# Rotary embedding: two DMA pieces merged with their neighbours, and two PSUM banks per ScalarE copy

## The chip, the cores and the metric

The kernel runs on one core of one Trainium2 chip. The metric is the device time of one execution, in microseconds. Executions over 1.5% slower than the fastest of the same kernel are left out of the means. A ratio in this document is the mean time of one kernel's fast runs over the mean of the other's fast runs in the same rounds, so it is not quite the ratio of the medians that stand beside it.

## The reference

```python
# x: (8, 2048, 8, 64) float32; cos, sin: (2048, 32) float32
x1, x2 = x[..., :32], x[..., 32:]
out1 = x1 * cos - x2 * sin          # cos, sin broadcast over batch and heads
out2 = x1 * sin + x2 * cos
return np.concatenate([out1, out2], axis=-1)
```

The kernel reads 33.5 MB of `x` and 0.5 MB of tables, and writes 33.5 MB.

## The kernel before

Each of the 8 batches is one SBUF tile of 128 partitions by 8192 floats (4 MB, 32 KB a partition), and five such tiles rotate. A batch is worked on in four units of 1 MB, some of them cut in halves. For a unit, GpSimd (POOL) makes `t2`, the products with the sine, and VectorE (DVE) makes `t1`, the product with the cosine; then DVE adds them in place. That is kind A. In kind B, TensorE adds the two through the identity matrix into PSUM, and ScalarE (ACT) copies the sum back; in kind C, DVE makes both products, and TensorE and ScalarE add them in the same way. Kinds B and C take the first unit of batches 1 to 5.

```python
    o_pool = ctx.enter_context(tc.tile_pool(name="op", bufs=2, space=PSUM))
    ...
    def load(b):
        xt = xpool.tile([P, ROW], f32, tag="xt", name=f"xt{b}")
        for lo, n in spans([UNIT, UNIT, 2 * UNIT] if b == 0 else [ROW]):
            keep(nc.sync.dma_start(out=xt[:, lo : lo + n], in_=xv[b, :, lo : lo + n]))
            ...  # the tables are loaded after the first piece
    ...
        if kind == "A":
            keep(nc.vector.tensor_add(out=xt, in0=t1, in1=t2))
        elif kind == "B":
            for j in range(n // C):                       # C = 512, one PSUM bank
                o = o_pool.tile([P, C], f32, tag="o")
                cs = slice(j * C, (j + 1) * C)
                nc.tensor.matmul(o, eye, t1[:, cs], start=True, stop=False)
                nc.tensor.matmul(o, eye, t2[:, cs], start=False, stop=True)
                keep(nc.scalar.copy(xt[:, cs], o))
    ...
    def pieces(b):                                        # what is computed at a time
        if b == 0:
            return [2 * HD, 2 * HD, UNIT, UNIT, UNIT]     # UNIT = 4 * HD
        if b == last:
            return [UNIT, UNIT, UNIT, 2 * HD, 2 * HD]
        return [UNIT] * 4

    def shares(b):                                        # what is stored at a time
        if b == 0:
            return [HD, 7 * HD, 2 * UNIT]
        if b == last:
            return [2 * UNIT, UNIT, UNIT]
        return [ROW]
```

## Time and profile before

| | before |
|---|---|
| time, median | 163.35 us (163.27 to 163.38) at first; 163.33 over 6 runs |
| span of the profiled run | 161.4 us |
| DVE, POOL busy | 140.1 us, 139.0 us |
| TensorE (PE), ACT busy | 46.4 us, 14.4 us |
| bytes moved, mean rate | 67.65 MB, 419 GB/s |

A busy share is a mean over the span. The 16 DMA engines each carry 8 of the 128 partitions and end at slightly different times, and the span ends with the last of them.

### The profile page before, as it was taken

The page shows a single profiled execution, that of the slowest core. Times are in us where ns is not written, and L with a number is a line of the kernel's source. Part 1 is how long each engine was busy: PE and PEld are TensorE (multiplying, and loading weights), DVE is VectorE, ACT ScalarE, POOL GpSimd, SP SyncE. Part 2 cuts the span into 40 slices and gives each one's busy share as a digit, 9 for nine tenths or more (in the row PEclk, how much of TensorE's full clock was granted, in tenths as well). Part 3 has the DMA queues.
Part 4 walks back from the last instruction along what each step waited for, and adds up shares of the span by engine and source line. Part 5 has one row for each costly group of instructions (what it writes and reads, how often), then busy time and mean ns, then how long its engine had stood idle before and what let it go on. Part 6 is the DMA issues. An engine that isn't in the chain of part 4 may idle for free.

```text
span 161.4 us, 467 instructions
## 1 busy us (share of the span) xinstructions
PE 46.4 (29%) x80; PEld 18.5 (11%) x80; DVE 140.1 (87%) x66; ACT 14.4 (9%) x24; POOL 139.0 (86%) x70
## 2 busy tenths in 40 slices
PE   0000000498008960893029912980000000000000
PEld 0000000133003420340014401430000000000000
DVE  0468899999999999999999999999899998999900
ACT  3200000013000220032001210140000000000000
POOL 1299999999999899998996999998999979999200
PEclk9999999999955696599755985799555555555555
DMA  5999999899999999999999999999999999999995
GB/s 181 418 445 464 449 430 390 373 427 499 406 390 447 430 487 390 447 438 414 447 422 430 447 416 438 447 406 447 455 392 455 447 398 455 438 406 455 410 398 231
DMA packets 3458, 67.65 MB, mean 419 GB/s; under 512 B 384, under 2 KB 384, under 8 KB 768
## 3 DMA queue, kind: packets, MB, share of 16 engines
q1 hardware_dynamic: 1728, 34.08, 49.8%
q10 hardware_dynamic: 1728, 33.56, 48.4%
q14 instruction: 2, 0.02, 0.0%
HBM read 34.08 MB, written 33.55 MB: 419 GB/s over the span
## 4 chain that ended last, share of the span: by engine, by line
DMA 46%; DVE 37%; POOL 9%; issue 2%; SPq 1%; DVEq 0%; POOLq 0%; ACTq 0%
DMA xt<-in_x_dram 24%; DVE t L128 18%; DMA out_dram<-xt 18%; DVE xt L135 17%; POOL t L121 9%; DMA sin_sb<-in_sin_dram 3%; DVE t L145 1%; SPq L69 0%; SPq L67 0%; DVEq L135 0%; POOLq L121 0%; ACTq L74 0%
## 5 line engine op out<-in xcount | busy, mean ns | idle before, releaser
L121 POOL TENSOR_TENSOR t<-xt,sin_sb 128x1024 f32<-128x1024 f32 (+1 forms) x32 | 70.4, 2200 | 10.7 <-DMA sin_sb<-in_sin_dram 5.7
L128 DVE TENSOR_TENSOR t<-xt,cos_ps 128x2048 f32<-128x2048 f32 (+1 forms) x34 | 73.4, 2166 | 0.8
L121 POOL TENSOR_TENSOR t<-xt,nsin 128x1024 f32<-128x1024 f32 (+1 forms) x32 | 70.4, 2200 | 0.0
L135 DVE TENSOR_TENSOR xt<-t,t 128x2048 f32<-128x2048 f32 (+1 forms) x29 | 62.2, 2144 | 6.2 <-POOL t L121 3.7
L140 PE MATMUL o<-t,eye 128*128 128x512 f32 x24 | 17.1, 803 | 25.2 <-DVE t L128 25.2
L156 PE MATMUL o<-t,eye 128*128 128x512 f32 x16 | 10.9, 781 | 36.8 <-DVE t L128 36.8
L141 PE MATMUL o<-t,eye 128*128 128x512 f32 x24 | 15.0, 710 | 0.0
L142 ACT COPY xt<-o 128x512 f32<-128x512 f32 x12 | 7.0, 586 | 46.5 <-PE o L141 46.5
L140 PEld LDWEIGHTS o<-t,eye 128*128 128x128 f32 x24 | 5.6, 247 | 33.5 <-issue 33.5
L161 ACT COPY xt<-o 128x512 f32<-128x512 f32 x8 | 4.7, 586 | 42.6 <-PE o L157 42.6
L156 PEld LDWEIGHTS o<-t,eye 128*128 128x128 f32 x16 | 3.6, 247 | 41.7 <-POOL t L121 30.6
L141 PEld LDWEIGHTS o<-t,eye 128*128 128x128 f32 x24 | 5.9, 248 | 8.5 <-issue 8.5
L92 DVE COPY cos_ps<-cos_sb 128x512 f32<-128x512 f32 x1 | 0.7, 695 | 6.2 <-DMA cos_sb<-in_cos_dram 6.2
L157 PE MATMUL o<-t,neye 128*128 128x512 f32 x8 | 4.9, 714 | 0.2 <-DVE t L145 0.2
L145 DVE TENSOR_TENSOR t<-xt,sin_ps 128x2048 f32<-128x2048 f32 x2 | 4.6, 2279 | 0.0
L157 PE MATMUL o<-t,eye 128*128 128x512 f32 x8 | 4.1, 592 | 0.0
L157 PEld LDWEIGHTS o<-t,neye 128*128 128x128 f32 x8 | 1.8, 239 | 3.6 <-issue 3.6
L157 PEld LDWEIGHTS o<-t,eye 128*128 128x128 f32 x8 | 1.5, 190 | 1.9 <-issue 1.9
L89 ACT ACT_TABLE_LOAD x1 | 1.3, 1283 | 0.7 <-PEq L204 0.7
L89 ACT ACTIVATE nsin<-sin_sb 128x512 f32<-128x512 f32 x1 | 0.6, 629 | 4.9 <-DMA sin_sb<-in_sin_dram 4.9
L90 ACT COPY sin_ps<-sin_sb 128x512 f32<-128x512 f32 x1 | 0.6, 580 | 0.0
L79 POOL MEMSET eye<- 128x128 f32 x1 | 0.2, 205 | 0.3 <-POOLq L204 0.3
(6 smaller groups left out, 1.0 us busy)
## 6 DMA issues: line engine op xcount, KB each, us to landing
xt<-in_x_dram SPq DMA_DIRECT2D x7, 4096.0 KB, 38.9
out_dram<-xt ACTq DMA_DIRECT2D x6, 4096.0 KB, 28.3
out_dram<-xt ACTq DMA_DIRECT2D x2, 2048.0 KB, 18.9
xt<-in_x_dram SPq DMA_DIRECT2D x2, 1024.0 KB, 6.0
xt<-in_x_dram SPq DMA_DIRECT2D x1, 2048.0 KB, 11.5
out_dram<-xt ACTq DMA_DIRECT2D x2, 1024.0 KB, 8.7
out_dram<-xt ACTq DMA_DIRECT2D x1, 1792.0 KB, 20.4
cos_sb<-in_cos_dram SPq DMA_DIRECT2D x1, 256.0 KB, 5.0
```

The source lines that it names most:

```text
L89: keep(nc.scalar.mul(nsin, sin_sb, -1.0))
L92: keep(nc.vector.tensor_copy(cos_ps, cos_sb))
L121: nc.gpsimd.tensor_mul(out=t2u[:, :, u, :].rearrange("p (r h) d -> p r h d", h=H), in0=xu[:, :, 1 - u, :].rearrange("p (r h) d -> p r h d" ...
L128: nc.vector.tensor_mul(out=t1.rearrange("p (r k d) -> p r k d", r=nr, d=Dh), in0=xk, in1=rep(cos_ps[:, r0 : r0 + nr, :], 2 * H),)
L135: keep(nc.vector.tensor_add(out=xt, in0=t1, in1=t2))
L140: nc.tensor.matmul(o, eye, t1[:, cs], start=True, stop=False)
L141: nc.tensor.matmul(o, eye, t2[:, cs], start=False, stop=True)
L142: keep(nc.scalar.copy(xt[:, cs], o))
L145: nc.vector.tensor_mul(out=t2.rearrange("p (r k d) -> p r k d", r=nr, d=Dh), in0=xk, in1=rep(sin_ps[:, r0 : r0 + nr, :], 2 * H),)
L156: nc.tensor.matmul(o, eye, t1u[:, gs, u, :], start=True, stop=False)
L157: nc.tensor.matmul(o, eye if u else neye, t2u[:, gs, 1 - u, :], start=False, stop=True)
L161: nc.scalar.copy(xu[:, gs, u, :], o.rearrange("p (g d) -> p g d", d=Dh))
```

## The change

Its intent is fewer transfers and fewer instructions: one piece less at the front, one less at the end, and half as many ScalarE copies, each of two PSUM banks. The two single-bank buffers become one of two banks. All eight banks were already in use.

```diff
-    o_pool = ctx.enter_context(tc.tile_pool(name="op", bufs=2, space=PSUM))
+    o_pool = ctx.enter_context(tc.tile_pool(name="op", bufs=1, space=PSUM))
...
-        for lo, n in spans([UNIT, UNIT, 2 * UNIT] if b == 0 else [ROW]):
+        for lo, n in spans([UNIT, 3 * UNIT] if b == 0 else [ROW]):
...
-            for j in range(n // C):
-                o = o_pool.tile([P, C], f32, tag="o")
-                cs = slice(j * C, (j + 1) * C)
-                nc.tensor.matmul(o, eye, t1[:, cs], start=True, stop=False)
-                nc.tensor.matmul(o, eye, t2[:, cs], start=False, stop=True)
-                keep(nc.scalar.copy(xt[:, cs], o))
+            for j in range(n // (2 * C)):
+                o = o_pool.tile([P, 2 * C], f32, tag="o")
+                for k in range(2):
+                    cs = slice((2 * j + k) * C, (2 * j + k + 1) * C)
+                    oc = o[:, k * C : (k + 1) * C]
+                    nc.tensor.matmul(oc, eye, t1[:, cs], start=True, stop=False)
+                    nc.tensor.matmul(oc, eye, t2[:, cs], start=False, stop=True)
+                keep(nc.scalar.copy(xt[:, 2 * j * C : 2 * (j + 1) * C], o))
...        (kind C likewise: one copy for each half of the unit)
-            return [2 * UNIT, UNIT, UNIT]
+            return [3 * UNIT, UNIT]
```

More of the change, by code (lines that the diff above doesn't have):

```diff
@@ L152, in rotate @@
             for u in range(2):
+                o = o_pool.tile([P, n // 2], f32, tag="o")
                 for j in range(n // 2 // C):
-                    o = o_pool.tile([P, C], f32, tag="o")
+                    oc = o[:, j * C : (j + 1) * C]
                     gs = slice(j * G, (j + 1) * G)
-                    nc.tensor.matmul(o, eye, t1u[:, gs, u, :], start=True, stop=False)
+                    nc.tensor.matmul(oc, eye, t1u[:, gs, u, :], start=True, stop=False)
                     nc.tensor.matmul(
-                        o, eye if u else neye, t2u[:, gs, 1 - u, :], start=False, stop=True
+                        oc, eye if u else neye, t2u[:, gs, 1 - u, :], start=False, stop=True
                     )
-                    keep(
-                        nc.scalar.copy(
-                            xu[:, gs, u, :], o.rearrange("p (g d) -> p g d", d=Dh)
-                        )
+                keep(
+                    nc.scalar.copy(
+                        xu[:, :, u, :], o.rearrange("p (g d) -> p g d", d=Dh)
                     )
+                )
     def pieces(b):
```

## The prediction

> **What bounds the kernel now.** I read the page first, for the engines, the slices, the DMA queues and the chain that ended last.
>
> ```profile
> PE 46.4 (29%) x80; PEld 18.5 (11%) x80; DVE 140.1 (87%) x66; ACT 14.4 (9%) x24; POOL 139.0 (86%) x70
> ...
> DMA  5999999899999999999999999999999999999995
> ...
> q1 hardware_dynamic: 1728, 34.08, 49.8%
> q10 hardware_dynamic: 1728, 33.56, 48.4%
> ```
>
> Two engines are near 87%, but the DMA line is at 9 in almost every slice, and the loads (q1) and stores (q10) together fill 98.2% of 16 engines' span. Of 161.4 us that is 158.5 us of packets in each DMA engine. The trace's packet records agree: their durations sum to 158.6 us for each of the 16 engines, the first data packet starts at 1.75 us and the last one ends at 160.25 us, a stretch of 158.5 us. So the DMA engines have no gap at all: **the kernel is bound by the transfer of 67.65 MB**, with 1.75 us of start before it and about 1.2 us of ending after it. The time reported, 163.35 us, is 1.9 us more than the span; I keep that offset.
>
> The chain of waits seems to say something else, since it goes through compute twice:
>
> ```profile
> DMA 46%; DVE 37%; POOL 9%; issue 2%; SPq 1%; DVEq 0%; POOLq 0%; ACTq 0%
> ```
>
> A chain names one thing at each step and does not say how much slack the others had. The slack is seen in the timeline and in the issue and packet records of each transfer. The load of batch 7 was issued at 92.68 us, when store 2 was complete, but its first packet moved only at 110.88, because loads were queued ahead of it: 18 us of slack. Stores likewise: batch 1's was issued at 46.79 and began at 53.9, batch 2's at 63.05 and 73.3, batch 6's at 133.48 and 139.9. Compute is therefore ahead of the transfers nearly everywhere.
>
> Then I read the waits of POOL, the engine that sets the pace of compute, and the windows of the end.
>
> ```profile
> POOL t L121 <- DMA sin_sb<-in_sin_dram: 5.7, 1, 5.7
> POOL t L121 <- DMA xt<-in_x_dram: 2.8, 3, 1.1
> POOL t L121 <- DVE xt L135: 1.8, 2, 1.3
> ```
>
> POOL waits for the tables once, and then three times about 0.9 us for a whole batch to land (batches 5, 6 and 7). It catches up with the loads only at the end; these 2.8 us are what a small delay at the front can be absorbed in.
>
> ```profile
> 140.00:145.00 5.00, 0.00 (x0) 0.00 (x0) 4.86 (x3) 0.00 (x0) 5.00 (x3) 0.50 1.06 459
> 145.00:148.20 3.20, 0.00 (x0) 0.00 (x0) 3.06 (x3) 0.00 (x0) 3.20 (x4) 0.50 0.95 410
> ...
> 149.60:153.30 3.70, 0.00 (x0) 0.00 (x0) 3.56 (x3) 0.00 (x0) 0.71 (x1) 0.50 0.99 425
> 153.30:156.00 2.70, 0.00 (x0) 0.00 (x0) 0.00 (x0) 0.00 (x0) 0.00 (x0) 0.50 0.96 410
> 156.00:158.00 2.00, 0.00 (x0) 0.00 (x0) 0.00 (x0) 0.00 (x0) 0.00 (x0) 0.50 1.00 422
> ```
>
> After the stretch come five busy columns (PE, PEld, DVE, ACT, POOL), the clock, the DMA share and GB/s. The DMA share is about 1 while the last batch is computed and after, so the stores have work queued until they end.
>
> **What the Trainium skill says.** (1) "DMA: Bandwidth & Descriptors", section "Bandwidth", has a 1 MB transfer at 78% of peak and a 16 MB one at 97%, with the rule to batch to at least 1 MiB. That would speak for fewer, larger pieces. This trace does not agree for queued transfers: an 8 KB packet (a 1 MB piece) takes 309 ns, a 16 KB one 611 and a 32 KB one 1213, so a piece costs about 8 ns a packet more, not 20%. The page's figure is of one transfer alone. (2) The same page, "Queues, rings and completion order", says that each engine goes round robin between the queues that have work, a packet at a time. The trace agrees: from 14.5 us load and store packets alternate, spaced 1.3 us while 2 KB stores face 32 KB loads. (3) "PSUM — Partial Sum Buffer", section "The four PSUM rules": a matmul's output stays in one bank of 512 fp32. The change keeps each matmul at 512 and lets only the copy cross banks; no trace yet shows such a copy. (4) "ScalarE: Activation LUTs", section "What ACT_TABLE_LOAD costs", gives an instruction with immediate operands as 186 ns plus 0.833 ns an element. For 512 that is 613 ns; the copies here take 586, so the measured time is a little lower.
>
> **The change part by part.**
>
> *First load, 1 and 3 MB.* Per engine it takes away 8 packets of 8 KB and 8 of 16 KB, 8 x 309 + 8 x 611 = 7360 ns, and adds 8 of 24 KB. Halfway between 611 and 1213 is 912 ns (my estimate), so 7296 ns: 64 ns less, and one semaphore packet of 9 ns less. **0.07 us of DMA time saved.** It also moves work: the second megabyte had landed at 9.0 us and POOL began on it at 11.89. The 3 MB will land where the 2 MB piece did, at 13.8 us. From landing to POOL's start took 0.6 us for batches 6 and 7 (111.75 to 112.35, 131.11 to 131.71), so POOL starts this unit at 14.4, **2.5 us late**, DVE likewise. The lines that will move are these:
>
> ```profile
> 11.89 2.33 POOL L121 TENSOR_TENSOR t<-xt,sin_sb 128x1024 f32<-128x1024 f32 x1
> ...
> 16.53 2.29 DVE L135 TENSOR_TENSOR xt<-t,t 128x2048 f32<-128x2048 f32 x1 [0.84 <-POOL t L121]
> ```
>
> What does the delay cost? The DMA engines have loads for batches 1 to 4 queued, so they do not pause. Stores of batch 0 come up to 2.5 us later, while the queues have 6 us or more of backlog from batch 1 on. The delay then shrinks at the three waits for loads, 2.8 us in all, so at batch 7 about nothing of it is left. **0 us on the end.**
>
> *Last store, 3 and 1 MB.* By the same arithmetic, 8 packets of 16 KB and 8 of 8 KB become 8 of 24 KB: **0.07 us saved**. It moves the issue of the first 2 MB from 143.42 to 148.14. Is anything else queued until then? Batch 6's store is, to between 149.6 (the first of the 16 engines to finish it) and 150.5 (the last). A transfer issued at 148.14 needs its time from issue to first packet: the first load took 1.0 us (0.74 to 1.75). It is there at about 149.15, some 0.45 us before the first engine runs dry and 1.3 us before the last. **0 us lost, with thin slack.** The last megabyte still goes out at 153.33 and is needed at 157.
>
> *Two banks per copy.* There were 20 copies of 512 columns at 586 ns, 11.7 us of ACT. There will be 10 of 1024. With the page's 0.833 ns for 512 more columns, one takes 586 + 427 = 1013 ns, 10.1 us in all: **1.6 us of ACT saved, on an engine 9% busy, so 0 us.** There is now one buffer of two banks instead of two of one, so PE waits for the copy after each pair of banks. A unit with PE had 4 tiles; it will have two rounds of 8 matmul records and a copy. PE loses one copy of 1.0 us in between, and the last copy is 0.4 us longer, plus whatever the clock costs that PE loses while it waits (853 ns a record in the first 5 us of a unit and 430 after). So such a unit ends 1.5 us later, at most some 5. The slack: PE ended batch 2's unit at 59.1, its store went out at 63.05, and the buffer that PE held is next needed by POOL two units on, again about 4 us later. **0 us on the end.**
>
> The sum: -0.07 - 0.07 + 0 + 0 = -0.15 us, rounded; 163.35 becomes **163.2 us**.
>
> **The rivals.** *A hole in the store queue at the end.* If a transfer takes much more than the 1.0 us seen for the first load from issue to first packet, the engines wait at 149.6 to 150.5. Against it stands that 1.0 us; for it that the first store was issued at 10.80 and moved its first packet at 14.51. But the loads were queued ahead in the same engines then, which they are not at the end. If 3.7 us held there too, the 3 MB would be there at 151.84 and the last engine, done at 150.48, would wait 1.4 us: some 164.6 us. With 2 us instead of 3.7 the last engine would not wait.
>
> *The late start carries to the end.* If POOL does not win its 2.5 us back, batch 7 ends up to 2.5 us later, the 3 MB goes out at 150.6 instead of 148.1, and the last engine has a hole of 150.6 + 1.0 - 150.5, about 1.1 us; 164.3 us. Against it: the three waits for loads that absorb it, and that late stores let loads run ahead for a while (round robin has fewer partners), which gives later batches their data earlier. Here the total of bytes decides, not their order.
>
> *PE as a new bound.* With one buffer PE could hold a t2 buffer past POOL's need. POOL starts already sit just at 93.0 us near PE's end of batch 4's unit (93.5), though what ended that wait by the semaphores was DVE, not PE. If the allocation of buffers now made POOL wait for PE, three units would cost up to 2 us each, and behind a backlog of stores of 6 to 10 us even this would mostly be hidden: at most 165.
>
> *Faster than the bytes.* If the fixed cost of a transfer were really 2 us (the section "Anatomy of one DMA" of the DMA page gives about that), two transfers less would be worth 4 us. But packets of following transfers already run with no gap here: that cost lies beside others' work. I give it 1%.
>
> **Range and chances.** Three runs of the kernel before lie within 0.11 us. The fast end is 163.2 less a few tenths, as if packets of 24 KB went better than estimated: 162.8. The slow end is a hole of half a microsecond at the end: 164.0. Two per cent would be 3.3 us; only two rivals together reach it on the slow side. So 0.01 faster, 0.97 the same, 0.02 slower.
>
> **What would show it right or wrong.** Right: 3170 packets in place of 3458 (two transfers of 128 + 16 packets less), the same bytes, DMA at 98% of the span; 24 KB packets near 912 ns; POOL's second megabyte at about 14.4 us after a wait of some 2.5 us for the load, and the waits at batches 5 to 7 gone or smaller; 10 copies of 128x1024 near 1.01 us; the last batch's DVE end within 0.5 us of 153.3. Wrong: a dip of the DMA share near 149 to 151 us (the first rival), a last DVE add after 155 us (the second), or POOL waiting for PE (the third). A time under 160 us would mean that I misread what bounds it.

## The result, and the profile after

The changed kernel took 163.80 us (median of 6 runs, 163.71 to 164.04) against 163.33 us before (163.27 to 164.00 in the same rounds). The ratio is 1.0025, with a 95% interval of 1.0008 to 1.0042. So it is the same within 2%, and about 0.4 us slower.

The page of the changed kernel, its engines, slices, queues and chain:

```profile
PE 50.0 (31%) x80; PEld 18.7 (12%) x80; DVE 140.1 (86%) x66; ACT 12.8 (8%) x14; POOL 139.0 (86%) x70
...
DMA packets 3170, 67.65 MB, mean 418 GB/s; under 512 B 352, under 2 KB 352, under 8 KB 736
...
DVE 75%; DMA 8%; POOL 6%; issue 6%; SPq 1%; DVEq 0%
```

ACT is 1.6 us less busy with 10 copies in place of 20, and there are 288 packets less, both as foreseen. The chain has changed its character. Before, it went through a store and a load (DMA 46%) and reached compute again only at batch 7; now three quarters of it are DVE, from the first batch to the last. DMA stands only at its start, and POOL comes in for 4.6 us after that and again at 100.16 us. The chain is followed back from the last instruction, which is DVE's last add; the stores that come after it are not in it. So it shows that DVE now has almost no slack, and not that DVE bounds the kernel.

Where it starts, in the timeline (start, duration, engine, line, instruction, and in brackets the idle time before it and what ended it):

```profile
14.33 2.32 POOL L121 TENSOR_TENSOR t<-xt,sin_sb 128x1024 f32<-128x1024 f32 x1 [2.33 <-DMA xt<-in_x_dram]
...
18.96 2.29 DVE L135 TENSOR_TENSOR xt<-t,t 128x2048 f32<-128x2048 f32 x1 [2.31 <-POOL t L121]
```

POOL waits 2.33 us for the 3 MB to land, and the add that was at 16.53 us is at 18.96, 2.43 us late. At batch 7, the same timeline of the kernel before:

```profile
131.71 2.34 POOL L121 TENSOR_TENSOR t<-xt,sin_sb 128x1024 f32<-128x1024 f32 x1 [1.08 <-DMA xt<-in_x_dram]
...
136.37 2.29 DVE L135 TENSOR_TENSOR xt<-t,t 128x2048 f32<-128x2048 f32 x1 [0.59 <-POOL t L121]
```

and of the changed one:

```profile
132.20 2.35 POOL L121 TENSOR_TENSOR t<-xt,sin_sb 128x1024 f32<-128x1024 f32 x1
...
138.08 2.29 DVE L135 TENSOR_TENSOR xt<-t,t 128x2048 f32<-128x2048 f32 x1 [0.20 <-DVE t L128]
```

POOL has won nearly all of its delay back: it starts batch 7 only 0.49 us later than before, and no longer waits for the load. DVE has not: its add is at 138.08 instead of 136.37, 1.71 us late. The 3 MB are therefore issued at 149.86 us and not at 148.14, as the same timeline has it a little later:

```profile
149.86 0.34 ACTq L74 DMA_DIRECT2D out_dram<-xt  x1
```

The windows of the end show what that does (length, five busy columns, clock, DMA share, GB/s):

```profile
148.20:149.60 1.40, 0.00 (x0) 0.00 (x0) 1.40 (x1) 0.00 (x0) 1.40 (x3) 0.50 0.92 398
149.60:153.30 3.70, 0.00 (x0) 0.00 (x0) 3.53 (x4) 0.00 (x0) 1.23 (x2) 0.50 0.75 319
153.30:156.00 2.70, 0.00 (x0) 0.00 (x0) 1.60 (x2) 0.00 (x0) 0.00 (x0) 0.50 1.02 437
```

The DMA share was 0.99 in the window from 149.60 to 153.30 before and is 0.75 now: a hole. The trace's packet records give its size: between the end of batch 6's store (149.5 to 150.7 us, by engine) and the first packet of the 3 MB at 150.70, an engine stands idle for 0.75 us in the mean. No such hole exists before.

A hole of 0.75 us and a loss of 0.47 us in the medians have to be brought together. By the packet records, the mean completion of the 16 DMA engines moved from 159.72 to 160.59 us, by 0.87. The latest engine was 0.52 us behind that mean before and is 0.10 behind it now, because an engine that was behind had less of a hole to wait in: the first to finish batch 6's store, at 149.5 us, waited 1.3 us, the last, at 150.7, hardly at all. So the last completion moved from 160.24 to 160.70, by 0.46 us.

### The profile page after: what moved, and what is told of

Read it like the earlier page. It is cut to its first block, busy times and chain, and to the rows that moved or that the text cites. A ratio compares the mean times of both kernels' runs of the same rounds, so it can differ in the third digit from the quotient of the medians.

```text
span 162.0 us, 456 instructions
## 1 busy us (share of the span) xinstructions
PE 50.0 (31%) x80; PEld 18.7 (12%) x80; DVE 140.1 (86%) x66; ACT 12.8 (8%) x14; POOL 139.0 (86%) x70
## 2 busy tenths in 40 slices
DMA packets 3170, 67.65 MB, mean 418 GB/s; under 512 B 352, under 2 KB 352, under 8 KB 736
## 4 chain that ended last, share of the span: by engine, by line
DVE 75%; DMA 8%; POOL 6%; issue 6%; SPq 1%; DVEq 0%
DVE t L128 40%; DVE xt L135 33%; DMA xt<-in_x_dram 8%; POOL t L121 6%; DVE t L147 3%; DVEq L135 0%; SPq L69 0%; SPq L70 0%; SPq L67 0%
## 5 line engine op out<-in xcount | busy, mean ns | idle before, releaser
L159 PE MATMUL o<-t,eye 128*128 128x512 f32 x16 | 12.2, 852 | 40.6 <-DVE t L128 38.4
L142 PE MATMUL o<-t,eye 128*128 128x512 f32 x24 | 17.4, 817 | 22.7 <-DVE t L128 19.2
L143 PE MATMUL o<-t,eye 128*128 128x512 f32 x24 | 14.9, 710 | 0.0
L144 ACT COPY xt<-o 128x1024 f32<-128x1024 f32 x6 | 6.1, 1012 | 45.7 <-PE o L143 45.7
L164 ACT COPY xt<-o 128x1024 f32<-128x1024 f32 x4 | 4.0, 1012 | 50.3 <-PE o L160 50.3
L160 PE MATMUL o<-t,neye 128*128 128x512 f32 x8 | 6.4, 892 | 0.2 <-DVE t L147 0.2
L160 PE MATMUL o<-t,eye 128*128 128x512 f32 x8 | 4.1, 592 | 0.0
```

Source lines behind the costliest of these rows:

```text
L142: nc.tensor.matmul(oc, eye, t1[:, cs], start=True, stop=False)
L143: nc.tensor.matmul(oc, eye, t2[:, cs], start=False, stop=True)
L144: keep(nc.scalar.copy(xt[:, 2 * j * C : 2 * (j + 1) * C], o))
L159: nc.tensor.matmul(oc, eye, t1u[:, gs, u, :], start=True, stop=False)
L160: nc.tensor.matmul(oc, eye if u else neye, t2u[:, gs, 1 - u, :], start=False, stop=True)
L164: nc.scalar.copy(xu[:, :, u, :], o.rearrange("p (g d) -> p g d", d=Dh))
```

## The experiments

Twelve runs were made of eleven kernels (relief_again repeats relief_second), each timed in five rounds beside the kernel before. Six of them, with the kernel before and the changed one, are all eight combinations of the three parts. "Hole" is the mean idle time of a DMA engine between 145 and 157 us, and "mean end" the mean completion time of the 16 engines, both from the packet records of the profiled run. The median of before is that of the changed kernel's rounds; in the experiments' rounds it was 163.37 to 163.56. "Issued" is when the last batch's first piece was issued.

| kernel | fast median, us | ratio (95% interval) | issued | hole | mean end |
|---|---|---|---|---|---|
| before | 163.33 | 1 | 143.42 | 0.00 | 159.72 |
| changed | 163.80 | 1.0025 (1.0008 to 1.0042) | 149.86 | 0.75 | 160.59 |
| load_only | 163.63 | 1.0013 (0.9997 to 1.0029) | 145.06 | 0.00 | 159.75 |
| store_only | 163.29 | 0.9994 (0.9981 to 1.0006) | 148.20 | 0.00 | 159.65 |
| copy_only | 163.44 | 1.0005 (0.9988 to 1.0022) | 143.35 | 0.00 | 159.66 |
| load_store | 163.80 | 1.0024 (1.0012 to 1.0036) | 149.82 | 0.69 | 160.58 |
| store_copy | 163.41 | 0.9993 (0.9978 to 1.0008) | 148.10 | 0.00 | 159.63 |
| load_copy | 163.48 | 1.0000 (0.9981 to 1.0019) | 145.04 | 0.00 | 159.82 |
| store_4mb | 167.57 | 1.0252 (1.0234 to 1.0271) | 153.25 | 4.23 | 163.90 |
| load_121 | 163.49 | 0.9994 (0.9980 to 1.0007) | 148.15 | 0.00 | 159.69 |
| load_dose | 163.49 | 0.9996 (0.9982 to 1.0011) | 148.47 | 0.00 | 159.63 |
| dve_relief | 165.74 | 1.0137 (1.0119 to 1.0155) | 151.42 | 2.37 | 162.15 |
| relief_second | 164.27 | 1.0059 (1.0017 to 1.0102) | slow profile | | |
| relief_again | 163.81 | 1.0016 (0.9993 to 1.0039) | 148.99 | 0.06 | 159.90 |

The theory: the late load makes DVE late to the end, and the 3 MB store turns that lateness into a hole; it needs both. The rivals: one part alone does it, or the single PSUM buffer makes compute late.

**Each part alone, and load with store.** load_only takes the first line of this edit to the kernel before, store_only the second, load_store both; copy_only is the rest of the change without them.

```diff
-        for lo, n in spans([UNIT, UNIT, 2 * UNIT] if b == 0 else [ROW]):
+        for lo, n in spans([UNIT, 3 * UNIT] if b == 0 else [ROW]):
...
-            return [2 * UNIT, UNIT, UNIT]
+            return [3 * UNIT, UNIT]
```

> Only the first load is 1 and 3 MB; stores 2, 1, 1 and single-bank copies as before. My theory (a late start that VectorE never wins back, showing only through the 3 MB store): the last VectorE add ends near 155.0 us as in the changed kernel (before 153.3), but the 2 MB store is issued near 145.1 us, ahead of the end of batch 6's store at 149.6 to 150.5, so no hole: same time as before within 0.15 us (163.2 to 163.4). Rival that the late load alone is the cost (end moves with VectorE's end): 163.8 or more. Rival that the single two-bank buffer delays the end: VectorE's end back near 153.3 here.

Measured: DVE's last add ended at 154.9 us (it starts at 153.72 and takes 1.22), so the delay was there without the copy; no hole; the ends of the engines stayed where they were, 159.75 in the mean. The window that had 0.75 in the changed kernel:

```profile
149.60:153.30 3.70, 0.00 (x0) 0.00 (x0) 3.53 (x4) 0.00 (x0) 1.45 (x2) 0.50 1.03 443
```

The expected time was only partly met: the six runs went from 163.32 to 164.08, median 163.63, and the interval includes no difference. The profiled run was the slowest of them, 164.08 us, with one DMA engine 1.24 us behind the mean. That spread is looked at below.

> Only the last store is 3 and 1 MB. Theory: VectorE finishes the third unit at 148.1 us, the 3 MB are issued there and their first packet moves 0.84 us later, near 149.0, before the first DMA engine ends batch 6's store at 149.6: no hole, 163.2 to 163.4. Rival that a 3 MB store leaves a hole whenever it comes: 163.7 to 163.9.

Measured: 163.29 us, issued at 148.20, no hole:

```profile
149.60:153.30 3.70, 0.00 (x0) 0.00 (x0) 3.56 (x3) 0.00 (x0) 0.78 (x1) 0.50 1.02 438
```

The 3 MB store by itself costs nothing.

> Only the two-bank copies. Theory: ScalarE 1.6 us less busy, PE about as long or longer per unit, the last VectorE add at 153.3 us and the time unchanged, 163.2 to 163.4. Rival that PE's waiting for the one buffer is what makes VectorE late in the changed kernel: last VectorE add near 155 us.

Measured: 163.44 us, DVE's last add ended at 153.2 us. The two-bank copy by itself neither costs nor gains anything. The single PSUM buffer does not make compute late.

> The load and the store changed, copies as before. Theory: these two together are the whole loss: last VectorE add near 155 us, 3 MB store issued near 149.9, a hole of about 0.75 us per DMA engine before its first packet, 163.7 to 163.9. Rival of the two-bank copy: 163.3.

Measured: 163.80 us, issued at 149.82, a hole of 0.69 us. These two parts are the whole loss. The two-bank copy is cleared.

**Two parts of the change at a time, the third undone.** In store_copy the first line of the edit above is undone in the changed kernel, in load_copy the second.

> The changed kernel with the first load back to 1, 1 and 2 MB. Theory: VectorE's last add back near 153.3 us, the 3 MB issued near 148.1, no hole, 163.2 to 163.45. Rival that store and two-bank copy together cost something: 163.7 or more.

Measured: 163.41 us, issued at 148.10, no hole.

> The changed kernel with the last store back to 2, 1 and 1 MB. Theory: VectorE's last add stays near 155.0 us but no DMA engine runs dry, so the mean end of the 16 engines is 159.7 to 159.8 us as before and the time 163.2 to 163.7, the spread coming from one late DMA engine, which differed by 0.7 us between profiles. Rival that the late end of VectorE costs by itself: mean end of the engines 160.5 or later.

Measured: 163.48 us, mean end 159.82, no hole. DVE was as late as in the changed kernel, and the time was that of the kernel before:

```profile
137.99 2.29 DVE L135 TENSOR_TENSOR xt<-t,t 128x2048 f32<-128x2048 f32 x1 [0.20 <-DVE t L128]
```

A late DVE alone costs nothing; the smaller pieces of the last store had covered it.

**A larger dose of the hole.** In the kernel before:

```diff
-            return [2 * UNIT, UNIT, UNIT]
+            return [4 * UNIT]
```

> The kernel before with the last batch stored as one 4 MB piece: a larger dose of the hole. Theory: issued at 153.33, first packet 0.84 us later at 154.2, after batch 6's store ended at 149.95 in the mean: a hole of 4.2 us per engine, then 8 packets of 1.213 us, last packet near 164.0 and, with the 3.1 us from last packet to reported time of the changed kernel, 167.1 us. Rival that the queue was filled in another way or that fewer pieces help: 163.3.

Measured: 167.57 us, with a hole of 4.23 us and the last completion at 163.99, both as expected. The windows:

```profile
149.60:153.30 3.70, 0.00 (x0) 0.00 (x0) 3.48 (x3) 0.00 (x0) 0.64 (x1) 0.50 0.00 0
153.30:156.00 2.70, 0.00 (x0) 0.00 (x0) 0.00 (x0) 0.00 (x0) 0.00 (x0) 0.50 0.91 388
```

For more than 3 us nothing moves. The first packet came at 154.10, 0.84 us after the issue at 153.25, the same as in the changed kernel (149.86 to 150.70). From the last completion to the time reported the profiled run took 3.5 us and not the 3.1 I had assumed; that 0.4 us is not explained. The three profiles with a relief, below, have 3.4 to 3.5 us too, and the other ten 3.0 to 3.1.

**How late is too late.** Two other splits of the first load, in the changed kernel:

```diff
-        for lo, n in spans([UNIT, 3 * UNIT] if b == 0 else [ROW]):
+        for lo, n in spans([UNIT, 2 * UNIT, UNIT] if b == 0 else [ROW]):     # load_121
+        for lo, n in spans([UNIT, 10 * HD, 2 * HD] if b == 0 else [ROW]):    # load_dose
```

> The changed kernel with the first batch loaded as 1, 2 and 1 MB. Theory: the 2 MB land near 11.3 us, GpSimd goes on at 11.9 to 12.0 without a wait, no delay, last add near 153.3 us, no hole: 163.2 to 163.45 although the last store is still 3 and 1 MB. Rival that any change of the load's split costs: 163.8.

Measured: 163.49 us, ratio 0.9994; POOL went on at 11.97 us without a wait, the 3 MB were issued at 148.15, no hole. The time fell 0.04 us outside what I had expected, here and in load_dose, as the kernel before was at 163.56 in these rounds.

> The changed kernel with the first batch loaded as 1, 2.5 and 0.5 MB: about half the delay. Theory: the 2.5 MB land near 12.5 us, GpSimd starts near 13.0, 1.1 us late; some 0.7 us of it is won back as in the changed kernel, so the last add ends near 153.7, the 3 MB are issued near 148.5 and come before batch 6's store ends: no hole, 163.2 to 163.45. Rival of a cost in proportion to the delay: 163.5 to 163.6.

```profile
12.93 2.32 POOL L121 TENSOR_TENSOR t<-xt,sin_sb 128x1024 f32<-128x1024 f32 x1 [1.13 <-DMA xt<-in_x_dram]
```

Measured: 163.49 us, ratio 0.9996, issued at 148.47, no hole. A wait of 1.13 us leaves no hole, one of 2.33 us leaves one of 0.75. By the holes, the cost has a threshold and is not in proportion to the delay. The times alone hardly tell: in proportion, the ratio would be about 1.0012 (1.13 / 2.33 of the 0.0025), and the interval ends at 1.0011.

**Giving DVE its time back.** In the changed kernel, one more add is given to TensorE and ScalarE. The first try takes batch 6's first unit, the second and third its second unit.

```diff
-    for b, kind in ((1, "C"), (2, "B"), (3, "C"), (4, "B"), (5, "B")):
+    for b, kind in ((1, "C"), (2, "B"), (3, "C"), (4, "B"), (5, "B"), (6, "B")):   # dve_relief
...
+    kinds[(6, UNIT)] = "B"                                    # relief_second, relief_again
```

> The changed kernel, with the add of batch 6's first unit given from VectorE to TensorE and ScalarE, which frees 2.3 us of VectorE before batch 7. Theory: VectorE wins its 1.7 us back, batch 7 is then paced by GpSimd, its last add ends near 153.8 us instead of 155.0, the 3 MB are issued near 148.7 and arrive before batch 6's store ends: no hole, 163.2 to 163.5. Rival that GpSimd, not VectorE, carries the delay, or that the 3 MB load itself costs: unchanged at 163.8.

This failed: 165.74 us. The timeline shows a new wait that I had not foreseen:

```profile
123.06 2.29 DVE L135 TENSOR_TENSOR xt<-t,t 128x2048 f32<-128x2048 f32 x1 [2.17 <-POOL t L121]
...
125.43 2.33 POOL L121 TENSOR_TENSOR t<-xt,sin_sb 128x1024 f32<-128x1024 f32 x1 [2.40 <-DVE xt L135]
```

DVE skips an add, runs ahead and waits for POOL; then POOL waits for that very add to give a `t2` buffer free. TensorE still holds another of the three `t2` buffers for its unit. POOL loses 2.40 us, the 3 MB are issued at 151.42, and the hole grows to 2.37 us. The program of this run has the reason: it gives the third unit of batch 6 the same `t2` buffer, at the same address, as the second, and lets it wait for the second's add. The third buffer, which TensorE had finished reading near 113.4 us, is kept for the fourth unit. So it is the order in which buffers are handed out that costs the wait, with one of the three idle. A fourth buffer could not be tried, as the four ask for 32 KB a partition and 24.8 KB were left.

> A second try at freeing VectorE in the changed kernel: batch 6's second unit, not its first, is added by TensorE and ScalarE, so that by the order of buffers GpSimd has a free one after it. Theory: GpSimd runs without the 2.4 us wait of the first try, VectorE wins its delay back, the last add ends near 153.8 us, the 3 MB are issued near 148.7, no hole: 163.2 to 163.5. Rival that the delay is GpSimd's or that the 3 MB load costs by itself: 163.8 or more.

Its profile (166.93 us) is not compared; the five runs that count as fast went from 163.77 to 166.22. So it was run again:

> The second relief of VectorE again, because its first profile fell in the slow state (166.93 us, loads of batches 6 and 7 landing 1 to 2 us late) and cannot be compared. Theory, unchanged: in a fast profile GpSimd starts batch 7 near 132.2 us, VectorE's last add ends near 153.8, no hole. Its fast runs of 163.8 to 164.6 us speak against it; if they come again, the profile is to show whether the hole is still there (then the delay is not won back by freeing VectorE) or whether one or a few DMA engines are late (then it is the spread that also the kernel before shows).

Its timeline (the line numbers are two higher in this kernel):

```profile
127.66 2.29 DVE L137 TENSOR_TENSOR xt<-t,t 128x2048 f32<-128x2048 f32 x1 [1.97 <-POOL t L123]
...
137.21 2.29 DVE L137 TENSOR_TENSOR xt<-t,t 128x2048 f32<-128x2048 f32 x1 [0.20 <-DVE t L130]
```

Measured: the wait of POOL is gone, and DVE, having caught POOL up, waits 1.97 us for it; its add in batch 7 is at 137.21 instead of 138.08. The 3 MB are issued at 148.99, and the hole is 0.06 us instead of 0.75. This was the purpose, and it shows that DVE's lack of slack carried the delay. The time did not follow: 163.81 us in the median (163.67 to 164.22; one run of 166.31 is left out), no better than the changed kernel. The mean end fell from 160.59 to 159.90, but the latest engine is 0.50 us behind the mean again instead of 0.10, so the last completion came only 0.29 us earlier, at 160.41. From there to the time reported the profiled run took 3.5 us, where the changed kernel took 3.1: the unexplained 0.4 us of store_4mb again, and it hides the gain. With 3.1 it would have been 163.5 us (my estimate). As a repair it is worth nothing; the early split of the load (load_121, load_dose) or the early store (load_copy) does the same with less.

**The spread.** The kernel before itself gave 163.25 to 164.13 us in fast runs, more than the effect in question. In the packet records the mean end of the engines is steady (159.63 to 159.82 in the eight kernels without a hole, the one before included), while the latest engine is 0.5 to 1.2 us behind it. Each run shows two 8 KB packets on the instruction queue (q14), near 96 to 100 and near 116 to 119 us. Each takes 309 ns, and in the six profiles (before, changed, and the first four experiments) a 32 KB load packet that starts within 5 ns of its end takes some 1.75 us after the first and 1.43 after the second, in place of 1.21. In load_only's profile the latest engine went from 0.40 us behind the mean at 92 us to 1.28 at 111 us, across the first of them. A fetch that falls on an engine already behind would explain the run to run spread; no run here separated that, so it stays argued.

No kernel beat both. The lowest ratios, 0.9993 and 0.9994, are below 1 by less than their intervals.

## Why the prediction was right or wrong

The time lay in the range, 163.8 in 162.8 to 164.0, and the class was right. That is partly luck: the central value, 163.2, was a gain of 0.15 us, and the loss that came fits only because the slow end allowed for a hole of half a microsecond, and it came by a path that the prediction had argued against. One of its own signs of being wrong came, the dip of the DMA share at the end, and one of being right did not: the last add ended at 155.0 us and not within 0.5 us of 153.3. By its steps:

- **What bounds it.** Right. The DMA engines have no gap before, and every hole put into them came back in their mean end: holes of 0.75 us in the changed kernel, 2.37 in dve_relief and 4.23 in store_4mb moved it by 0.87, 2.43 and 4.18 us.
- **Packets saved.** Right in count and size: 3170 packets, 912 ns for a 24 KB load packet as estimated. The 24 KB stores took 922 ns in the mean of the changed kernel and 913 in store_only. What 0.15 us would have saved is below what the runs can tell: store_only's mean end is 0.07 us earlier than before, its time the same.
- **The two-bank copy.** Right. 1012 ns against 1013 predicted, and no effect on the time. A unit of TensorE, to the end of its last copy, took 11.7 us in batch 4 instead of 10.4, 1.3 us more against the 1.5 predicted.
- **The late start.** The size at the front was right: a wait of 2.33 us for 2.5 predicted, POOL at 14.33 for 14.4.
- **The step that failed** is "The delay then shrinks at the three waits for loads, 2.8 us in all, so at batch 7 about nothing of it is left. 0 us on the end." The three waits are in batches 4, 6 and 7 (0.93, 0.79 and 1.08 us; the prediction says 5, 6 and 7), and in the changed kernel all three are gone; as POOL then waits 0.9 us longer for a buffer in batch 4, it is 0.49 us late at batch 7. That much was nearly right. But I had counted the waits of POOL alone. The add needs DVE too, and after the first batch DVE waited only 0.33, 0.53 and 0.59 us, in batches 5, 6 and 7, and the first of these stands in the changed kernel too. That leaves 1.12 us. Of these, 0.40 remain in the changed kernel as two waits of 0.20 behind DVE's own product. So DVE wins back 0.72 us: 2.43 - 0.72 = 1.71 us, as the traces have it. In the last batches a unit takes DVE 4.73 us (138.08 to 142.81) and POOL 4.56 (134.50 to 139.06), so DVE cannot win back anything on POOL there.
- **The store's slack** was rightly called thin, and the time from issue to first packet was even better than assumed, 0.84 us for 1.0. The 3.7 us of the first rival did not come. With the store on time (store_only, store_copy) there is no hole, as the step said; it failed only because the step before it had failed. The second rival named the right path and came out at 164.3 us for the whole 2.5 us; with 1.71 us left the changed kernel took 163.8.
- **The third rival**, TensorE as a bound, is cleared by copy_only and load_store. POOL's longer wait for a buffer in batch 4 (2.2 us for 1.3) is in load_only too, so it comes from the late start.
- **The fourth rival**, a fixed cost of 2 us a transfer, did not come: with two transfers less the time rose. The section that it names describes transfers issued by GpSimd; these are issued by the sync and scalar engines.

## What to carry to other kernels

In a kernel bound by transfers, merging pieces saved some 8 ns a packet here, and it can cost the whole time that the last piece comes after the queue has run dry; check each piece's issue time, plus the time from issue to first packet, against the end of what is queued before it. When a delay is to be absorbed by slack, take the slack of every engine on the path, not of the one that waits most; here POOL had 2.8 us and DVE 0.7. Two changes that each cost nothing that the runs could tell can cost together, so test the pair.

## What the Trainium skill lacked or had wrong

- "DMA: Bandwidth & Descriptors", section "Latency and other measured facts", gives about 600 ns to the first byte for transfers issued by the sync or scalar queue. In four profiles here in which DMA engines had run out of stores, the first packet came 0.84 to 0.85 us after the start of the issue (149.86 to 150.70, 153.25 to 154.10, 151.42 to 152.26, 148.99 to 149.84), which is 0.5 us after the issue's own 0.34 us. The page does not say from where it counts.
- The same page, section "Bandwidth", lacks the case of pieces queued behind one another (its table is of transfers issued from GpSimd): here a 1 MB piece runs at 309 ns per 8 KB packet, the rate of 32 KB packets (1213 ns) within 2%, not at 78%.
- The same page, section "Queues, rings and completion order", says that row 14 is internal to the runtime, and no page gives what its packets cost the transfers beside them: here two 8 KB packets of q14 in a run, 309 ns each, and a 32 KB packet next to each that takes 1.75 or 1.43 us instead of 1.21.
- "ScalarE: Activation LUTs", section "What ACT_TABLE_LOAD costs", has the slope right for a copy out of two PSUM banks: (1012 - 586) / 512 = 0.832 ns an element for its 0.833. Its fixed part of 186 ns, given for ACTIVATE, is 160 for these COPY instructions (586 - 512 x 0.832).
